# A mixture of four softmaxes on one core: stores of units 0 to 21 issued by GpSimd instead of ScalarE and SyncE

## The chip, the core and the metric

The kernel runs on one core of a Trainium2 chip. Its time is the device time in microseconds (us) of one execution. Before the change the median of three runs is 787.08 us (786.73 to 787.19). A core has TensorE (PE in the profile), VectorE (DVE), ScalarE (ACT), GpSimd (POOL) and SyncE (SP), each with its own stream of instructions, and 16 DMA engines that move data between HBM and SBUF. An instruction that starts a DMA stands in the stream of the engine that issues it; the transfer then stands in a queue of that engine, and all queues are served by the same 16 DMA engines.

## The reference

For each of 32 x 128 rows there are four heads of 4096 logits and four prior logits. Each head's softmax is weighted with the softmax of the priors, and the four are added:

```python
prior_probs = softmax(prior)                 # (32, 128, 4)
mixture = sum over h of prior_probs[..., h, None] * softmax(logits[..., h, :])
```

Input is 32 x 128 x 4 x 4096 float32 (268.4 MB), output 32 x 128 x 4096 float32 (67.1 MB).

## The kernel before

**Units and slots.** A unit is one of the 32 batches: 128 rows, one per partition, four heads of 4096 float32. `ring` in SBUF has 12 slots of one head each, so it holds three units. Head `h` of unit `u` stands in slot `4u + h` modulo 12 (line 101), so unit `u + 2` takes the slots of unit `u - 1`.

**One unit.** For each head, DVE takes the row maximum (`peak`, word M, line 123), ACT the exponential with its sum (`exp`, E, line 128), DVE the reciprocal of the sum (`recip`, R, line 134). For heads 0 to 2, POOL makes a diagonal matrix of the weights (`diagonal`, G, line 137) and PE adds head times weight into PSUM (`weigh`, X, line 146). Head 3 takes two ways. In its first half (column blocks 0 and 1 of four) DVE adds it, weighted (weight C, line 153), to the PSUM sum (`add_last`, A, line 163). In its second half POOL scales it (Z, line 157), ACT copies the PSUM sum into the slot of head 1 (`evac`, V, line 182), and POOL adds the two (`add_scaled`, P, line 185, 128 x 1024 each). All four quarters of the result land in the slot of head 3, and `store` (S, line 120) writes that slot, 2048 KB, to HBM.

**The order.** Nothing is scheduled automatically: strings of words give the program order, and each engine gets its own instructions in that order. A word is an operation, its digits, a prime for the unit before, `+2` for two units on. `STEADY` (lines 27 to 30) runs for units 0 to 23, and the rest of `ORDER` is written out by hand. In `STEADY` the additions that end unit `u - 1` are `P23' P34'`; then come `E1 X0`, the store `S'` and the two loads of unit `u + 2`: `L03+2` (heads 0 to 2, one DMA of 6144 KB) and `L34+2` (head 3, 2048 KB). All loads are issued by SP (line 115). Stores of units 2 to 21 are issued by ACT, all others by SP (line 119).

**Who holds whom.** `L03+2` goes into slots that the last addition of unit `u - 1` read, so it waits for `P34'`. `L34+2` goes into the slot that `S'` is writing out, so it waits until that store has landed. Both stand in SP's stream in this order, so a late `L34` also holds the next unit's `L03`.

Of the kernel before, what the change touches and what calls it, by code (L numbers as in the profile page):

```python
# [24 lines left out]

FIRST = "L01 L12 L23 L34"
STEADY = (
    "M0 E0 R3' C3' Z324' M1 R0 G0 A01' A12' V23' P23' V34' P34' E1 X0 S' L03+2 L34+2 "
    "M2 E2 R1 G1 X1 M3 E3 R2 G2 X2 "
)  # L30
ORDER = [STEADY] * 24
# [36 lines left out]
def kernel(  # L68
# [6 lines left out]
    nc = tc.nc  # L75
# [31 lines left out]
    def home(u, a, b):  # L107
        return slot(u, 3, a, b)
# [7 lines left out]
            h += n  # L116

    def store(u, a=0, b=4):
        queue = nc.scalar if 2 <= u < 22 else nc.sync
        queue.dma_start(out=out[u, :, a * C : b * C], in_=home(u, a, b))  # L120

    def peak(u, h):
# [61 lines left out]
    def add_scaled(u, a, b):  # L184
        nc.gpsimd.tensor_add(home(u, a, b), slot(u, 1, a, b), slot(u, 3, a, b))  # L185

    step = {
        "L": load, "S": store, "M": peak, "E": exp, "R": recip, "G": diagonal, "X": weigh,
        "C": weight, "Z": scale, "A": add_last, "B": add_head, "T": add_both, "V": evac,
        "P": add_scaled, "W": add_second,  # L190
# [67 lines left out]
```

## Time and profile before

| what | before |
|---|---|
| median of three runs | 787.08 us |
| the profiled execution | 787.09 us, its span 785.4 us |
| busy share PE / DVE / ACT / POOL | 87% / 82% / 70% / 37% |
| moved by DMA | 335.90 MB, mean 428 GB/s |
| SP waiting for a store to land, ahead of a load | 419.1 us in 28 waits |
| SP waiting for the last addition, ahead of a load | 159.6 us in 21 waits |
| granted PE clock, mean | 0.964 |

Times in the profile are of one execution, counted from the span's start; the 1.7 us between span and time lie outside the recorded instructions. A share is a part of the span. "Idle" beside an instruction is the time that its engine sat still just before it, with what ended the wait. In the queue table a share is the time that the queue's packets took, added up and divided by 16 engines' span; queue q1 is SP's, q10 ACT's. The time "to landing" of a DMA runs from its issue to the last of its 16 completion marks.

### The profile page before, as it was taken

Reading aid. Unit: us, or ns where it says so; the run is one execution under the profiler, and the core shown is the slowest. Engines: PE = TensorE matmul, PEld = TensorE weight load, DVE = VectorE, ACT = ScalarE, POOL = GpSimd, SP = SyncE. Lnnn points to the kernel's source line nnn. Section 1 sums busy time; section 2 is a strip of 40 time slices with the busy share of each in tenths; the row PEclk is TensorE's granted clock in tenths of the full one; section 3 lists DMA queues with packets and bytes.
Section 4 is the critical chain, followed back from the end, with each engine's and each line's share of the span. In section 5 each row is a group of like instructions: output and inputs, shape, how many; then the busy total and the mean of one; then the engine's idle time right before and its main releaser. Section 6 shows DMA issues by size and latency. Waiting matters only on the chain.

```text
span 785.4 us, 4589 instructions
## 1 busy us (share of the span) xinstructions
PE 681.8 (87%) x1508; PEld 293.0 (37%) x1508; DVE 645.1 (82%) x327; ACT 547.5 (70%) x326; POOL 293.8 (37%) x243
## 2 busy tenths in 40 slices
PE   0959998989999888998989989898888998899996
PEld 0424433333344333433334334343333443344342
DVE  6489977897778977779877798777888887979895
ACT  2557867867668666686676776766857668779883
POOL 0033323433134332334322343323430544277892
PEclk9989999999989999999999989999989899999999
DMA  9999999999999999999999999999999999999998
GB/s 378 456 411 426 429 436 413 433 437 441 435 416 431 448 436 421 434 424 436 444 429 430 420 436 438 439 427 421 432 449 421 440 408 431 451 412 431 429 429 351
DMA packets 15335, 335.90 MB, mean 428 GB/s; under 512 B 1712, under 2 KB 1712, under 8 KB 2256
## 3 DMA queue, kind: packets, MB, share of 16 engines
q1 hardware_dynamic: 12384, 293.61, 87.1%
q10 hardware_dynamic: 2928, 42.01, 12.5%
q8 instruction: 12, 0.20, 0.1%
q14 instruction: 11, 0.09, 0.0%
HBM read 268.50 MB, written 67.11 MB: 427 GB/s over the span
## 4 chain that ended last, share of the span: by engine, by line
DMA 58%; DVE 12%; PE 10%; POOL 10%; ACT 5%; issue 4%; SPq 0%; POOLq 0%; ACTq 0%
DMA ring<-in_logits_dram 58%; DVE nmax L123 11%; PE acc L146 10%; POOL ring L185 7%; ACT ring L128 3%; ACT ring L182 2%; POOL ring L179 1%; POOL ring L157 1%; POOL diag L137 1%; DVE ring L163 0%; SPq L115 0%; DVE rden L134 0%; SPq L120 0%; POOLq L185 0%; POOLq L137 0%
## 5 line engine op out<-in xcount | busy, mean ns | idle before, releaser
L146 PE MATMUL acc<-ring,diag 128*128 128x512 f32 x1508 | 681.8, 613 | 96.6 <-ACT ring L182 62.0
L123 DVE TENSOR_REDUCE nmax<-ring 128x1 f32<-128x4096 f32 x128 | 563.0, 4409 | 114.6 <-DMA ring<-in_logits_dram 114.6
L128 ACT ACTIVATE ring<-ring,nmax 128x4096 f32<-128x4096 f32 x128 | 474.6, 3708 | 202.5 <-DVE nmax L123 202.1
L146 PEld LDWEIGHTS acc<-ring,diag 128*128 128x128 f32 x1508 | 293.0, 196 | 484.5 <-issue 358.2
L185 POOL TENSOR_TENSOR ring<-ring 128x1024 f32<-128x1024 f32 x68 | 160.1, 2374 | 20.1 <-ACT ring L182 11.2
L137 POOL TENSOR_SCALAR diag<-ident,rden,pp 128x128 f32<-128x128 f32 x96 | 43.0, 448 | 239.7 <-DVE rden L134 239.7
L153 POOL TENSOR_TENSOR wght<-rden,pp 128x1 f32<-128x1 f32 x33 | 6.3, 190 | 210.4 <-DVE rden L134 210.4
L182 ACT ACTIVATE ring<-acc 128x1024 f32<-128x1024 f32 x68 | 66.7, 1012 | 17.9 <-PE acc L146 13.8
L157 POOL TENSOR_SCALAR ring<-ring,rden,pp 128x2048 f32<-128x2048 f32 (+3 forms) x35 | 74.2, 2121 | 9.0 <-DVE rden L134 8.7
L163 DVE SCALAR_TENSOR_TENSOR ring<-ring,wght,acc 128x1024 f32<-128x1024 f32 x60 | 74.2, 1269 | 3.3 <-PE acc L146 2.3
L134 DVE RECIPROCAL rden<-dsum 128x1 f32<-128x1 f32 x128 | 19.3, 153 | 10.2 <-ACT ring L128 10.2
L128 ACT ACTIVATION_READ_ACCUMULATOR ring<-ring,nmax 128x1 f32 x128 | 24.2, 189 | 0.0
L179 POOL TENSOR_TENSOR ring<-ring 128x1024 f32<-128x1024 f32 x5 | 11.8, 2367 | 0.1
L213 DVE TENSOR_REDUCE pmax<-pr 32x128 f32<-32x512 f32 x1 | 0.7, 674 | 5.3 <-DMA pr<-in_prior_dram 5.3
L215 ACT ACTIVATE pr<-pr 32x512 f32<-32x512 f32 x1 | 0.6, 628 | 4.2 <-DVE pr L214 4.2
L163 DVE SCALAR_TENSOR_TENSOR ring<-ring,wght 128x1024 f32<-128x1024 f32 x2 | 2.5, 1280 | 0.3 <-POOL wght L153 0.3
L215 ACT ACT_TABLE_LOAD x1 | 1.3, 1283 | 1.2 <-PEq L242 1.2
L222 DVE STREAM_TRANSPOSE pp<-pn 32x128 f32<-32x128 f32 x4 | 1.2, 302 | 0.1
L216 DVE TENSOR_REDUCE pmax<-pr 32x128 f32<-32x512 f32 x1 | 0.7, 674 | 0.7 <-ACT pr L215 0.7
L218 DVE TENSOR_TENSOR pn<-pr,pmax 32x512 f32<-32x512 f32 x1 | 1.0, 1016 | 0.0
L217 DVE RECIPROCAL pmax<-pmax 32x128 f32<-32x128 f32 x1 | 0.9, 941 | 0.0
L214 DVE TENSOR_TENSOR pr<-pr,pmax 32x512 f32<-32x512 f32 x1 | 0.7, 680 | 0.0
(6 smaller groups left out, 0.9 us busy)
## 6 DMA issues: line engine op xcount, KB each, us to landing
ring<-in_logits_dram SPq DMA_DIRECT2D x27, 6144.0 KB, 34.3
ring<-in_logits_dram SPq DMA_DIRECT2D x43, 2048.0 KB, 25.5
out_dram<-ring ACTq DMA_DIRECT2D x20, 2048.0 KB, 16.1
out_dram<-ring SPq DMA_DIRECT2D x11, 2048.0 KB, 14.0
out_dram<-ring SPq DMA_DIRECT2D x4, 512.0 KB, 5.5
pr<-in_prior_dram ACTq DMA_DIRECT2D x1, 64.0 KB, 4.5
ring<-in_logits_dram SPq DMA_DIRECT2D x1, 39.5
```

What stands on the lines that cost most here:

```text
L123: nc.vector.tensor_reduce(out=nmax[:, u, h : h + 1], in_=slot(u, h), op=ALU.max, axis=AX.X, negate=True)
L128: nc.scalar.activation(slot(u, h), slot(u, h), AF.Exp, bias=nmax[:, u, h : h + 1], accum_out=dsum[:, u, h : h + 1],)
L134: nc.vector.reciprocal(rden[:, u, h : h + 1], dsum[:, u, h : h + 1])
L137: nc.gpsimd.tensor_scalar(out=diag[:, u % 2, h], in0=ident, scalar1=rden[:, u, h : h + 1], scalar2=pp[:, h, u : u + 1], op0=ALU.mult, op1= ...
L146: nc.tensor.matmul(acc[:, k * W : (k + 1) * W], lhsT=diag[:, u % 2, h], rhs=e[:, k * W : (k + 1) * W], start=h == 0, stop=h == H - 2 or (u ...
L153: nc.gpsimd.tensor_mul(wght[:, u, h : h + 1], rden[:, u, h : h + 1], pp[:, h, u : u + 1])
L157: nc.gpsimd.tensor_scalar(out=e, in0=e, scalar1=rden[:, u, h : h + 1], scalar2=pp[:, h, u : u + 1], op0=ALU.mult, op1=ALU.mult,)
L163: nc.vector.scalar_tensor_tensor(out=o, in0=slot(u, h, a, b), scalar=wght[:, u, h : h + 1], in1=more, op0=ALU.mult, op1=ALU.add,)
L179: nc.gpsimd.tensor_add(e, e, slot(u, 2, a, b))
L182: nc.scalar.activation(slot(u, 1, a, b), acc[:, a * C : b * C], AF.Copy)
L185: nc.gpsimd.tensor_add(home(u, a, b), slot(u, 1, a, b), slot(u, 3, a, b))
L215: nc.scalar.activation(pr, pr, AF.Exp)
```

## The change

Two edits. The queue of a store becomes GpSimd's for units 0 to 21, and SP's for the rest; before, units 0 and 1 were SP's and units 2 to 21 ACT's. And the word `S'` moves up in `STEADY`, from behind `E1 X0` to right behind `P34'`.

```diff
-    "M0 E0 R3' C3' Z324' M1 R0 G0 A01' A12' V23' P23' V34' P34' E1 X0 S' L03+2 L34+2 "
+    "M0 E0 R3' C3' Z324' M1 R0 G0 A01' A12' V23' P23' V34' P34' S' E1 X0 L03+2 L34+2 "
     "M2 E2 R1 G1 X1 M3 E3 R2 G2 X2 "
...
-        queue = nc.scalar if 2 <= u < 22 else nc.sync
+        queue = nc.gpsimd if u < 22 else nc.sync
         queue.dma_start(out=out[u, :, a * C : b * C], in_=home(u, a, b))
```

In the built program PE's and DVE's streams are the same as before. ACT's loses its 20 stores and keeps the rest in the same order. SP's loses the stores of units 0 and 1, and its loads keep their order. In POOL's stream 22 stores come in, each behind the second `P` of its unit and ahead of the next unit's `G1 G2`; a store waits there for POOL's own addition and for DVE's additions. `E1` and `X0` are on ACT and PE, which the moved word no longer touches; the stores of units 22 and later stay where they were in SP's stream.

## Prediction

> **What bounds the kernel now.** I read the slices and the queue table first, since SP waits 419.1 us for stores and one should know whether that starves anything.
>
> ```profile
> DMA  9999999999999999999999999999999999999998
> ...
> q1 hardware_dynamic: 12384, 293.61, 87.1%
> q10 hardware_dynamic: 2928, 42.01, 12.5%
> q8 instruction: 12, 0.20, 0.1%
> q14 instruction: 11, 0.09, 0.0%
> ```
>
> All 40 slices but the last are full. The four queues' packets add up to 87.1 + 12.5 + 0.1 + 0.0 = 99.7% of 16 engines' span: 783.0 of 785.4 us. The DMA engines are idle for about 2.4 us, mostly before the first packet and after the last, so the time is the sum of the packets. No slice of an engine's idleness is left to fill, and whatever a packet costs more or less passes straight to the end. The chain of waits agrees: 58% of it is loads in flight.
>
> Per byte: SP's queue takes 0.871 x 785.4 = 684.1 us for 293.61 MB (429.2 GB/s), ACT's 98.2 us for 42.01 MB (427.9 GB/s). A store costs the same on a queue of its own as among the loads. The counts tell the packet: ACT's queue has 20 stores x 128 rows + 32 rows of the prior + 21 x 16 completion marks = 2928. One row of 16 KB is one packet.
>
> Then one steady unit in the timeline, around the end of its last addition, engine by engine:
>
> ```profile
> 313.53 4.70 POOL L185 TENSOR_TENSOR ring<-ring 128x1024 f32<-128x1024 f32 x2
> 319.89 0.45 POOL L137 TENSOR_SCALAR diag<-ident,rden,pp 128x128 f32<-128x128 f32 x1 [1.66 <-DVE rden L134]
> ```
> ```profile
> 317.63 0.20 ACT L128 ACTIVATION_READ_ACCUMULATOR ring<-ring,nmax 128x1 f32 x1
> 318.26 0.36 ACTq L120 DMA_DIRECT2D out_dram<-ring  x1
> 319.67 3.71 ACT L128 ACTIVATE ring<-ring,nmax 128x4096 f32<-128x4096 f32 x1 [1.84 <-DVE nmax L123]
> ```
> ```profile
> 334.94 0.33 SPq L115 DMA_DIRECT2D ring<-in_logits_dram  x1
> ```
> ```profile
> 342.49 0.33 SPq L115 DMA_DIRECT2D ring<-in_logits_dram  x1
> ```
>
> The addition ends at 313.53 + 4.70 = 318.23; ACT, through with E1 at 317.83, issues the store 0.03 us later. The store already goes right behind the addition. L34, which waits for it to land, leaves 16.7 us later, at 334.94; the next L03 leaves at 342.49, when the next addition has ended, so L34 stands 7.5 us ahead of need. How deep the queue is, the issue table shows:
>
> ```profile
> ring<-in_logits_dram SPq DMA_DIRECT2D x27, 6144.0 KB, 34.3
> ring<-in_logits_dram SPq DMA_DIRECT2D x43, 2048.0 KB, 25.5
> out_dram<-ring ACTq DMA_DIRECT2D x20, 2048.0 KB, 16.1
> ```
>
> At 429.2 GB/s 6144 KB take 14.7 us, yet they land after 34.3: each L03 queues behind some 10 us of loads, while stores take the rest. SP's long wait for the store passes while loads are in flight.
>
> **The change part by part.**
>
> *22 stores to GpSimd's queue.* They are 22 x 2.097 = 46.1 MB, 107.8 us of all engines at ACT's price. Twenty stood on ACT's queue at that price already; two move from SP's (2 x 4.886 = 9.77 us) to it (9.80): 0.03 us. No row shows a packet of GpSimd's queue, and that is the one unknown that counts. From below: the 48 KB load packets take 1815 ns in the trace's packet records (605 per 16 KB), a 16 KB row 611; 6 ns less on 22 x 128 / 16 = 176 packets per engine is -1.1 us. From above: if GpSimd cuts a row into pieces, the last four stores have 4 KB packets of 159 ns (4 x 159 = 636, +25 ns a row, +4.4 us), and the prior has 2 KB packets of 84 ns (672, +61, +10.7 us). I take ACT's price, since the rows, the source and the target are the same: 0.
>
> *The store's issue.* It goes 0.03 us behind the addition now and cannot go sooner; on POOL it also waits for POOL's own result. So no store leaves earlier. An issue takes 0.33 us on SP and 0.36 on ACT; on POOL no row shows it, and I bound it by 0.33 and by POOL's longest instruction, 2.37 us (the addition), nearer the first, since it too only issues. If it lands up to 2.4 us later, L34 still leaves 5 us before the next L03, with 10 us of loads queued: 0. Without that cover a late store would hold L34, and behind it in SP's stream the next L03.
>
> *What stands behind it on POOL.* G1 waits for DVE's reciprocal and starts 1.66 us after the addition. An issue over that delays G1, X1 on PE, and in the end the next addition. PE waits 96.6 us in all, 3.1 per unit, so a hold of up to about 4.8 us fits into the period. PE is the cover; beyond it each us costs 21 us.
>
> *ACT without stores.* Each frees 0.36 us, but E2 waits for the maximum until 319.67 anyway (1.84 us idle): 0.
>
> *Units 0 and 1.* SP issued these stores in front of the loads of units 3 and 4, at 56.49 and 79.54. On POOL they share the engines with the loads instead of going first. Unit 3's L34, which left at 68.85 after the store landed, leaves some 5 us later: the store's eight packets per engine now alternate with loads. The 6144 KB ahead of it take until 83, so nothing runs dry. If the first store took far longer, the second would already be queued behind it and fill the engines. 0.
>
> *The end.* From unit 22 on, stores and loads keep their order on SP: 0.
>
> Sum: 787.09 + 0.03 = 787.1 us; the profiled execution is within 0.01 us of the median, so no correction.
>
> **Rivals.** A difference under 0.2% (1.6 us) I call the same; that is about what a measurement of this kernel can tell.
>
> *Dearer packets (slower).* 1.6 us is 1.5% of 107.8, that is 9 ns on each 16 KB row: from there on the change shows. With 4 KB pieces it would be 787.1 + 4.4 = 791.5, with 2 KB 797.8. Against it: both queues in the trace move whole rows. For it: the trace has no store of GpSimd's. Small pieces would also get a smaller turn beside 48 KB load packets; the store would then land only when SP's loads run out. If no store were then queued to fill the gap, each unit would lose about 1.8 us (0.46 from the last mark at 334.48 to the load, 0.33 issue, 1.0 from the first issue at 0.79 to the first packet at 1.81): 20 x 1.8 + 4.4, so 827.5. But the next store leaves POOL 24.2 us after this one and fills it.
>
> The Trainium skill, "DMA: Bandwidth & Descriptors" (SWDGE vs HWDGE vs iDMA), says that a DMA issued from GpSimd has its descriptors computed by software and that a packet there is preferably at most 4096 B, the boundary at which an engine changes queues. By that the sum would be 791.5; the packets of the trace's two queues do not keep to 4096 B, and no run here shows GpSimd's.
>
> *Uneven engines (slower).* The sum holds for the slowest of the 16. Now they stay even: the first and last mark of a store lie 2.7 us apart at unit 1 (90.70, 93.39) and 2.9 at unit 21 (574.83, 577.72). If a GpSimd store cost one engine the time of one more small packet, 84 to 159 ns, 22 of them give 1.8 to 3.5 us: up to 790.6.
>
> The same page (Latency and other measured facts) says that engines 7 and 15 are usually slower, and guesses at the ports of the memory that holds GpSimd's descriptors. By it this case would come; the marks of before speak neither way, since no store there is GpSimd's.
>
> *POOL held (slower).* At a hold of 6 us, 1.2 over the cover: 787.1 + 21 x 1.2 = 812. It decides from 4.8 us, twice POOL's longest row.
>
> *Earlier loads (faster).* If stores landed sooner, SP's 419.1 us of waiting would shrink. But full engines pay for it: of the 2.4 us idle, 1.8 lie before the first packet. 0.6 plus the 1.1 of cheaper packets give 785.4 at best.
>
> *The change does nothing it says*: the issue moves by 0.03 us at most, so its second half indeed does nothing. That lies within the forecast.
>
> **How the numbers follow.** Forecast (same) 0.56, own range 786.0 to 788.6. Dearer packets 0.23 (4 KB 0.15, 2 KB 0.05, gaps 0.03); uneven engines 0.11; POOL held 0.05; faster 0.05. Slower 0.39, same 0.56, faster 0.05. The range takes in the forecast, the 4 KB pieces and the uneven engines (0.82): 786.0 to 793.0, the last 1.5 for the two together. The 2 KB pieces, the gaps and the held POOL stay outside.
>
> **What would show it.** A third data queue with 22 x 128 rows + 22 x 16 marks = 3168 packets and about 13.7%, ACT's all but gone, and all shares together still 99.7%: the forecast. More packets, or a share well over 13.7%: dearer packets. Shares that fall short of the span with empty DMA slices: gaps or uneven engines. G1 later than 1.7 us behind the addition, with PE idle over 97 us: POOL. I am wrong if the DMA row shows holes, since the whole argument is that it has none.

## The result, and the profile after

The changed kernel takes 789.67 us (median of seven runs, 789.16 to 790.28), the kernel before 786.92 beside it. The ratio is 1.0033, with a 95% interval of 1.0022 to 1.0045: 2.75 us slower. That lies inside the range 786.0 to 793.0, but it is not the "same" that was forecast as likeliest, and the cause is none of the rivals. That the range holds it is luck: its upper part stood for 4 KB pieces and uneven engines, and neither came. The profiled execution took 789.72 us, its span 788.0.

The slices and the queue table of the changed kernel first:

```profile
DMA  9999999999999999999999999999999999999997
...
q1 hardware_dynamic: 12096, 289.41, 85.7%
q0 software_dynamic: 3168, 46.14, 13.8%
q8 instruction: 12, 0.20, 0.1%
q14 instruction: 11, 0.09, 0.0%
q10 hardware_dynamic: 48, 0.07, 0.0%
```

GpSimd's queue is q0. It has exactly the forecast 3168 packets, so a row of 16 KB is one packet here too, and 13.8% of the span. All shares add up to 99.6%, and no slice looks empty. By this view the forecast held, and yet 2.6 us are gone. A 9 in the DMA row means 90% or more, and a tenth of a 20 us slice is 2 us: the view is too coarse for a loss of this size.

The steady unit, in the timeline of POOL (the store is now busy time of POOL):

```profile
314.95 4.69 POOL L185 TENSOR_TENSOR ring<-ring 128x1024 f32<-128x1024 f32 x2
319.94 0.61 POOL L120 DMA_DIRECT2D out_dram<-ring  x1 [0.30 <-POOL ring L185]
321.32 0.44 POOL L137 TENSOR_SCALAR diag<-ident,rden,pp 128x128 f32<-128x128 f32 x1 [0.77 <-DVE rden L134]
```

The store starts 0.30 us after the addition and holds POOL for 0.61; G1 starts 1.68 us behind the addition, before it was 1.66. The store lands 16.3 us after its issue instead of 16.1:

```profile
out_dram<-ring POOLq DMA_DIRECT2D x22, 2048.0 KB, 16.3
```

So the steady part runs as before. A table by stage says where the time went. Columns are the stretch in us, its length, busy time and count of PE, PEld, DVE, ACT and POOL, granted clock, DMA share and, last, GB/s. Before:

```profile
56.00:112.00 56.00, 56.00 (x131) 24.70 (x130) 48.26 (x25) 41.87 (x26) 17.89 (x17) 1.00 1.01 425
112.00:760.00 648.00, 581.13 (x1286) 249.37 (x1285) 543.27 (x270) 467.43 (x280) 256.27 (x205) 0.96 1.00 431
```

After:

```profile
56.00:112.00 56.00, 56.00 (x132) 24.81 (x131) 48.63 (x25) 41.85 (x26) 19.86 (x20) 1.00 1.00 410
112.00:760.00 648.00, 577.71 (x1280) 247.72 (x1279) 540.74 (x268) 465.12 (x277) 265.71 (x221) 0.97 1.00 432
```

From 112 us on the rate is the same. Between 56 and 112 us it falls from 425 to 410 GB/s: 15/425 x 56 = 2.0 us, all of it in the stretch in which the stores of units 0 and 1 go out. The chain of waits names the place; the longest pieces at its start, of the changed kernel:

```profile
42.42 4.43 DVE nmax L123
56.81 25.10 DMA out_dram<-ring
82.41 27.45 DMA ring<-in_logits_dram
```

Unit 0's store takes 25.1 us until SP, held by it, can go on. Before, unit 3's L34 and unit 4's L03 left one after the other, as SP's timeline shows:

```profile
68.85 0.33 SPq L115 DMA_DIRECT2D ring<-in_logits_dram  x1
79.93 0.43 SPq L115 DMA_DIRECT2D ring<-in_logits_dram  x1
```

In the changed kernel they leave together, the L34 at 81.97, 13.1 us later, and the L03 at 82.41, 2.5 us later:

```profile
81.97 1.60 SPq L115 DMA_DIRECT2D ring<-in_logits_dram  x2
```

The packet records (start, length, size and queue of every single DMA packet) tell why it is so slow. The store is issued at 56.81, its first packet starts at 61.66. About then the 16 KB packets of unit 2's last load run out (the packet of its last mark is at 62.7), and every packet of the store takes turns with one 48 KB packet of unit 3's load. An engine has eight of each: 8 x (1.815 + 0.611) = 19.4 us from 61.7, which is 81.1. Store and load end together; the packet of the store's last mark is at 81.4, and SP goes on 0.6 us behind it. SP, waiting for the store, has nothing else queued, so the loads' queue is empty at 81 us.

### The profile page after: what moved, and what is told of

Same layout as the page of the kernel before. It is cut to its first block, busy times and chain, and to the rows that moved or that the text cites. A ratio compares the mean times of both kernels' runs of the same rounds, so it can differ in the third digit from the quotient of the medians.

```text
span 788.0 us, 4615 instructions
## 1 busy us (share of the span) xinstructions
PE 680.2 (86%) x1508; PEld 292.3 (37%) x1508; DVE 645.1 (82%) x327; ACT 547.1 (69%) x326; POOL 307.1 (39%) x265
## 3 DMA queue, kind: packets, MB, share of 16 engines
q0 software_dynamic: 3168, 46.14, 13.8%
## 4 chain that ended last, share of the span: by engine, by line
DMA 65%; DVE 12%; POOL 10%; issue 6%; ACT 5%; PE 2%; SPq 0%; POOLq 0%
DMA ring<-in_logits_dram 62%; DVE nmax L123 12%; POOL ring L185 7%; DMA out_dram<-ring 3%; ACT ring L128 3%; ACT ring L182 2%; PE acc L146 2%; POOL ring L179 1%; POOL ring L157 1%; POOL diag L137 1%; DVE ring L163 0%; SPq L115 0%; SPq L120 0%; DVE rden L134 0%; POOLq L185 0%
## 5 line engine op out<-in xcount | busy, mean ns | idle before, releaser
L146 PE MATMUL acc<-ring,diag 128*128 128x512 f32 x1508 | 680.2, 612 | 100.4 <-ACT ring L182 61.1
L120 POOL DMA_DIRECT2D out_dram<-ring x22 | 13.6, 617 | 6.6 <-POOL ring L185 6.6
## 6 DMA issues: line engine op xcount, KB each, us to landing
out_dram<-ring POOLq DMA_DIRECT2D x22, 2048.0 KB, 16.3
```

Source lines behind the costliest of these rows:

```text
L146: nc.tensor.matmul(acc[:, k * W : (k + 1) * W], lhsT=diag[:, u % 2, h], rhs=e[:, k * W : (k + 1) * W], start=h == 0, stop=h == H - 2 or (u ...
```

## The experiments

Each kernel was timed beside the kernel before on the same chip. The explanation so far, a cost that comes once, at units 0 and 1, is called "start" below. Two theories stood against it: a price per store, and a fixed price of using GpSimd's queue. The diffs are against the changed kernel. Where they put stores back on ACT or SP (`e2_first_two_sync` to `e7_unit1_alone`), the word `S'` stands at its old place, behind `E1 X0`, as well.

**The changed kernel again** (`e1_again`).

> The changed kernel once more, for a second profile. Three theories of the +2.75 us (789.67 against 786.92). Start: units 0 and 1 cost about 1.9 us once (both queues run dry at 81 us, the restart makes first packets about 0.8 us longer; and load packets between 102 and 109 us are stretched by 1.0 us), closing costs 0.46 us once (the end after the last landing 1.53 us instead of 1.07). Per store: each GpSimd store costs 0.12 us (22 x 0.12 = 2.75). Fixed: any use of GpSimd's queue costs it all. All give 789.7 here; what is open is whether the stretched packets between 102 and 109 us come again. If they were chance, this profile lacks them.

Measured: 789.73 us against 787.10, ratio 1.0031 (1.0020 to 1.0042). The stretched packets came again: between 100 and 112 us the packets take 1.23 us per engine more than the median of their size; in the first profile 1.14, before the change 0.10. So they are not chance.

**Units 0 and 1 back on SP** (`e2_first_two_sync`), with 20 stores left to GpSimd.

```diff
-        queue = nc.gpsimd if u < 22 else nc.sync
+        queue = nc.gpsimd if 2 <= u < 22 else nc.sync
```

> GpSimd issues units 2 to 21, SP keeps units 0 and 1. Start: only the closing is left, 786.9 + 0.5 = 787.4, loads of units 3 and 4 issued at 57, 69, 80 and 94 us as before. Per store: 20 x 0.12, 789.4. Fixed: 789.7.

Measured: 787.35 against 787.10, ratio 1.0002 (0.9993 to 1.0011). Per store and fixed fall: twenty stores of GpSimd's cost nothing that can be measured, 0.9 us at most by the interval. The longer end that the expected 787.4 counts in is not there: this profile ends 0.97 us after the last landing.

**Units 0 and 1 alone on GpSimd** (`e3_first_two_alone`), ACT keeps the rest.

```diff
-        queue = nc.gpsimd if u < 22 else nc.sync
+        queue = nc.gpsimd if u < 2 else nc.scalar if u < 22 else nc.sync
```

> GpSimd issues units 0 and 1 alone, ACT keeps 2 to 21. Start: start and closing are both there, 789.3 to 789.7, and the restart at 81 us is seen. Per store: 2 x 0.12, 787.2. Fixed: 789.7.

Measured: 789.23 against 787.10, ratio 1.0027 (1.0016 to 1.0038), with 406 GB/s between 56 and 112 us. The two stores bring 2.1 of the 2.6 to 2.75 us. That is just under the expected 789.3, which counted a longer end in; here the end is 1.12 us, hardly more than the 1.07 before.

**The same two on ACT, no GpSimd store at all** (`e4_first_two_act`).

```diff
-        queue = nc.gpsimd if u < 22 else nc.sync
+        queue = nc.scalar if u < 22 else nc.sync
```

> No GpSimd store: ACT issues units 0 to 21 from the old place. Start, if any queue beside the loads' will do: the first store alternates with the 48 KB load packets, lands with them near 81 us, and 786.9 + 1.9 = 788.8. Start, if the later first packet of a GpSimd store is what matters: ACT's store is in time to alternate with the last 16 KB packets of unit 2, lands by 76 us, and 786.9 to 787.2. Per store and fixed: 786.9.

Measured: 788.23 against 787.10, ratio 1.0014 (1.0005 to 1.0023), single runs from 786.91 to 789.26; two of the eleven lost nothing. The median lies between the two expectations. In the profiled run, which took 788.74, ACT's first packet starts at 60.77 rather than 61.66, and the store's last mark stands at 79.9 instead of 81.4, at the edge of running dry. No store here is GpSimd's, so about 1.1 us of the cost (0.4 to 1.8 by the interval) comes from taking the store out of SP's queue. That the rest comes from GpSimd's later first packet is likely, but not shown.

**Unit 0 on GpSimd, unit 1 back on SP** (`e6_unit0_alone`).

```diff
-        queue = nc.gpsimd if u < 22 else nc.sync
+        queue = nc.gpsimd if u < 22 and u != 1 else nc.sync
```

> GpSimd issues unit 0 and units 2 to 21, SP keeps unit 1. Start theory: the store of unit 0 again lands with the load of unit 3 near 81 us, and now no second store stands in GpSimd's queue to fill the gap, since unit 1's stands in SP's stream behind the waiting load: all engines idle for 1.5 to 2.5 us near 82 us, slower than the changed kernel, 789.5 to 791.5. If the second store filled nothing: 788.8 to 789.7, as in the changed kernel. Per store and fixed, already unlikely: 789.5.

Measured: 791.66 against 787.01, ratio 1.0059 (1.0046 to 1.0071): slower than the changed kernel, though less is changed, and a little over the expected 791.5. Now nothing stands behind the late store, and the hole shows. The 4 us around it, first in the experiment, then in the changed kernel, then before:

```profile
80.00:84.00 4.00, 4.00 (x11) 1.80 (x10) 3.87 (x2) 3.78 (x4) 0.45 (x1) 1.00 0.38 111
80.00:84.00 4.00, 4.00 (x11) 1.85 (x10) 4.00 (x1) 3.40 (x2) 0.56 (x2) 1.00 0.78 287
80.00:84.00 4.00, 4.00 (x10) 1.72 (x10) 3.96 (x2) 3.70 (x3) 0.45 (x1) 1.00 0.77 328
```

The DMA share is 0.38, and by the packet records the engines are idle for 2.06 us between 76 and 100 us. (A packet counts where it starts, so in so short a stretch a share under 1 is not yet idle time; that is read from the packets.) In the changed kernel the share there is 0.78 (0.77 before) and the idle time 0.05: unit 1's store does fill the hole.

**Unit 1 on GpSimd, unit 0 back on SP** (`e7_unit1_alone`).

```diff
-        queue = nc.gpsimd if u < 22 else nc.sync
+        queue = nc.gpsimd if 1 <= u < 22 else nc.sync
```

> GpSimd issues units 1 to 21, SP keeps unit 0. Start theory: the store of unit 0 lands near 69 us as before, loads keep the engines full, 787.1 to 787.5. If it were unit 1's store that costs: 788.5 to 789.7.

Measured: 787.08 against 787.01, ratio 0.9999 (0.9990 to 1.0008). One store, unit 0's, carries the whole start.

**Unit 3's load cut by heads** (`e9_unit3_by_head`), all 22 stores on GpSimd. This tests the turns.

```diff
-            while h + n < to and place(u, h + n) == s + n:
+            while u != 3 and h + n < to and place(u, h + n) == s + n:
```

> The changed kernel, but unit 3's heads 0 to 2 are loaded by three DMAs of 2048 KB, rows of 16 KB, in place of one of 6144 KB, rows of 48 KB; the first of them may leave earlier, since its slot is free earlier. Start theory, with turns taken packet by packet: the store of unit 0 alternates with 16 KB packets, so it lands some 10 us after its first packet, near 73 us, the next load follows while loads are in flight, and the cost is gone: 787.1 to 787.6. If the late landing comes from GpSimd's way of issuing and not from the turns: 788.9 to 789.7 as in the changed kernel.

Measured: 787.27 against 787.01, ratio 1.0003 (0.9994 to 1.0011). The store's first packet starts as late as in the changed kernel (61.9), but beside 16 KB packets its last mark stands at 72.7, and SP's load behind it leaves at 73.16:

```profile
73.16 0.33 SPq L115 DMA_DIRECT2D ring<-in_logits_dram  x1
```

The rate between 56 and 112 us is back:

```profile
56.00:112.00 56.00, 56.00 (x129) 24.61 (x128) 49.58 (x25) 41.87 (x26) 19.95 (x20) 0.98 1.01 425
```

The late first packet alone is harmless; what costs is the turn beside packets three times as large. One thing more differs: the first of unit 3's three loads left at 29.56, the other two at 56.55 and 56.98. That does not explain the store's landing, since eight pairs of 16 KB packets take 8 x (0.611 + 0.611) = 9.8 us, which fits the 61.9 to 72.7.

**The word alone** (`e8_word_only`): `S'` moved, queues as before, so that ACT waits for the addition ahead of E1.

> The word moved and the queues as before: ACT issues units 2 to 21 right behind the addition, ahead of E1, so ACT stands still for the addition of 4.7 us, once per unit. It delays E1 by about 4.5 us; DVE has 4 us and PE 3 us idle per unit, and loads are 10 us deep. If that covers it: 787.1 to 787.6. If not, up to 1.5 us per unit: 815. (With GpSimd's queue the moved word changes nothing in the built program.)

Measured: 787.21 against 787.01, ratio 1.0001 (0.9992 to 1.0011). ACT waited for the addition 20 times, 81.7 us in all, and the kernel took no longer. So a wait of 4.1 us per unit is covered. The idle time of DVE ahead of the row maximum fell from 114.6 to 49.7 us, which fits it as part of the cover; more was not tried.

**Unit 4's load cut by heads** (`e10_unit4_by_head`), the same edit with `u != 4`. It asks about the stretched packets only.

> The changed kernel, but unit 4's heads 0 to 2 are loaded by three DMAs of 2048 KB, rows of 16 KB; unit 3's load is as in the changed kernel. This asks only about the second part of the cost, the last 48 KB packets of unit 4's load, stretched by about 1.1 us per engine between 102 and 109 us in both profiles of the changed kernel. The queues still run dry at 81 us, which leaves 0.8 to 1.0 us and the restart. If the stretch belongs to that one 6144 KB DMA: it goes, 788.0 to 788.6, and packets between 100 and 112 us are stretched by less than 0.3 us per engine. If it belongs to the time or to the rows that are read: it stays near 1.1 us, 789.2 to 789.8.

Measured: 789.81 against 787.66 on this chip, ratio 1.0028 (1.0017 to 1.0039). The expectations were counted from 786.9; by the 2.15 us over the kernel before, the time lies between the two and does not decide. Part of it is a hole of 1.0 us at 81 us, for unit 1's store was issued at 81.03 here, not at 79.51, too late to fill it. The packets decide: between 100 and 112 us they are still stretched by 0.86 us per engine, now those of 16 KB. So the stretch does not need one DMA of 6144 KB.

The stretch came in the four profiles in which an SP issue right after the dry point is long: 1.16 us at 82.41 in the changed kernel, 1.19, 1.18 and 1.51 in `e1_again`, `e3_first_two_alone` and `e10_unit4_by_head`; in all others no issue there takes over 0.44 us and the stretch is at most 0.36. And in all four the stretched packets are those of the load with the long issue: in `e10_unit4_by_head` unit 4's third load has all of the 0.86 us, the two issued just before it, in 0.37 and 0.44 us, have none. Why issue and stretch go together was not settled.

## Why the prediction was right and wrong, point by point

*What bounds the kernel: right.* The engines are full before and after, and a loss passes straight to the end: the rate from 112 to 760 us is the same, so the 2.0 us lost by 112 us are not made up. That they are full is shown by the 99.7% of the queue table, not by the 9s of the slices, which begin at 90%.

*22 stores at ACT's price: right.* 13.8% of 788.0 us is 108.7, forecast 107.8; the median 16 KB packet takes 611 ns on q0 as on the other queues. The rival of dearer packets falls. The Trainium skill's "DMA: Bandwidth & Descriptors" (SWDGE vs HWDGE vs iDMA) prefers packets of at most 4096 B on this path; this trace does not keep to that, with 2816 packets of 16384 B.

*The issue and what stands behind it on POOL: right.* 0.61 us is between the bounds 0.33 and 2.37; G1 starts 0.02 us later. PE's idle time, 96.6 us before, is 100.4 in this profile and 96.9 in the second one of the same kernel; with twenty stores on POOL (`e2_first_two_sync`) it is 96.0. The rival of a held POOL falls.

*Uneven engines: falls.* Twenty stores cost 0.9 us at most (`e2_first_two_sync`); by this rival's 84 to 159 ns each they would cost 1.7 to 3.2.

*The moved word: right.* `e2_first_two_sync` has the word at its old place; apart from the two stores, which stand on SP, its trace has the same instructions in the same order as the changed kernel's on all five engines (semaphore instructions left out).

*Units 0 and 1: wrong. This is the step that failed.* The prediction said that unit 3's L34 "leaves some 5 us later", that "nothing runs dry", and "If the first store took far longer, the second would already be queued behind it and fill the engines. 0." The L34 left 13.1 us later. The turns were in the prediction, but with the wrong neighbour: I let the store's packets start soon after its issue and pass beside the 16 KB packets of unit 2, and eight of these add 8 x 0.611 = 4.9 us. The store's packets started 4.9 us after the issue and met 48 KB packets alone, eight of which take 14.5 us. Where the neighbours are 16 KB packets (`e9_unit3_by_head`), the L34 does leave 4.3 us later, about as forecast. The row for a slow landing was there: the ACT stores land after 16.1 us in the steady part, where they too stand beside loads.

The other half of the sentence, that the second store would fill the engines, held: the engines were idle for 0.05 us, and for 2.06 us where that store was missing (`e6_unit0_alone`). But filling the hole is not free, and the 0 was wrong. Right at 81 us the first packets of unit 1's store take about 0.9 to 1.8 us instead of 0.611, and its last ones, at 86 us, up to 1.2. The packet records put 0.94 us per engine, beyond the median of each packet's size, on the stretch from 76 to 100 us (0.10 before) and 1.14 on 100 to 112 us (0.10 before). The sum is 1.9 us of the 2.0. So the late landing is shown with its cause; why packets are longer once the loads' queue has run dry is open.

*The end: off by 0.46 us.* The span ends 1.53 us after the last landing, before 1.07. The four profiles with 22 GpSimd stores need 1.41 to 1.54, the two with 21 need 1.32 and 1.33, all others 0.97 to 1.12, `e2_first_two_sync` with its 20 stores the least: it is no price of using the queue, as I had expected in the experiments. With 22, POOL pauses for 0.32 us ahead of its last drain; with 21, for 0.35 us ahead of its very last instruction; with 20 or fewer there is neither pause. What makes it was not tried.

The sum of what was found: 2.0 us at the start and 0.46 at the end of the 2.6 between the spans; 0.2 are left, within the spread of single runs.

The turns themselves stand in the Trainium skill too: the same page (Queues, rings and completion order) says that an engine goes round between queues packet by packet. The trace agrees, with turns of one row: 19.4 us for eight pairs of 48 and 16 KB, and a store whose last mark stands at 72.7 instead of 81.4 once the pairs are of 16 KB.

## What to carry to other kernels

Moving a transfer from the queue of the loads to one of its own does not only free the loads from it; it also changes its place in line, from "next" to "every other packet". If a wait hangs on it, work out its landing by packets: as many turns as it has packets, each with the packet that stands beside it. In this kernel it cost nothing in the steady part, where the loads' queue is deep, and 2.0 us at the start, where it ran empty. Another queue that fills the hole hides most of it in the busy share, so look at GB/s by stage.

## What the runs showed of the hardware that was not expected

A store's first packet started 4.9 us after its issue on GpSimd's queue (56.81 to 61.66) and 4.2 us on ACT's (56.60 to 60.77), with 16 KB load packets ahead of it. And after the queues had run dry, load packets some 20 us later were stretched: the last 16 packets of unit 4's 6144 KB load, one per engine, took 2.6 to 2.9 us each instead of 1.815. They came with a long issue of that same load (1.16 us); why is open.
